# Whole-block additions on VectorE, angles and decays behind z's first gated block, and another order of the GLA value products

## The chip, the cores and the metric

The kernel runs on one core of one Trainium2 chip. The metric is the device time of one execution in microseconds, as the median over runs. The five engines are TensorE (PE in the profile, PEld its weight loads), VectorE (DVE), ScalarE (ACT), GpSimd (POOL) and SyncE (SP), which here issues nearly all transfers.

## What is computed

One layer of a decoder trunk over 1024 tokens of width 1024, in fp32. A normalized input h is projected by one wide matrix; three mixers run on pieces of the projection (sliding-window attention, gated linear attention, or GLA, and a Mamba-2 scan, or SSD); their gated outputs are projected, merged with sigmoid gates and projected once more. Cut to what the change touches:

```python
h = rms_norm(x, norm_g)
proj = h @ w_in
(aq, ak, av, ag, gq, gk, gv, gg, gdown, sxbc, sdt, sz, mg) = jnp.split(proj, split_points, axis=-1)
q = apply_rope(rms_norm(aq.reshape(b, s, ATTN_HEADS, ATTN_HEAD_DIM), attn_q_norm), cos, sin)
k = apply_rope(rms_norm(ak.reshape(b, s, ATTN_KV_HEADS, ATTN_HEAD_DIM), attn_k_norm), cos, sin)
...
o_b = gated_linear_attention(gq, gk, gv, log_alpha)
dt = jax.nn.softplus((sdt + ssd_dt_bias).astype(jnp.float32))
y_c = ssd_scan(xh, dt, a_head, sb, sc)
y_c = gated_group_rms_norm(y_c, sz, ssd_out_norm, SSD_GROUPS)
```

## The kernel before

**Products.** fp32 products are made of three fp32r products each: a matrix is split into a rounded part (hi) and the remainder (lo), and hi*hi, lo*hi and hi*lo are summed in PSUM. `split` (line 259) makes the weights' parts `wh_...` (a cast, mostly on ScalarE, line 262) and `wl_...` (a subtraction, on VectorE or GpSimd, line 265). h itself is kept as hi and lo in four blocks, `hb["11"]`, `"12"`, `"21"` and `"22"`: the first digit is the half of the width, the second the half of the tokens.

**Seven products for eight.** Most wide projections multiply 2x2 blocks with seven block products (Strassen-Winograd) instead of eight. For that they need sums of h's blocks: `block_sums` (line 489) builds t1 = 12 - 11, t3 = 22 - 12 and t2 = 22 - t1, and the loop under `zp` (line 524) builds t4n = 21 - t2, each for four slices k of 128 rows. `whole` (line 480) adds hi and lo of a slice back to the full value; `block_diff` (line 483) subtracts two, has ScalarE cast the result to `ht_hi` (line 486) and VectorE form `ht_lo` (line 487). Twelve of the `whole` calls in `block_sums` and four of the eight under `zp` run on GpSimd, the other four on VectorE.

**Order of the stages.** Input and norm; keys and values (`ps_kv`); the first query projection (`dense_tm`, line 475); the second query projection, by slices of the weight (`dense_tm_by_k`, line 293, tiles `ps_tm`, `wh_tm`, `wl_tm`); the gate z (`dense_pair_tm`, line 376, called at line 530, tiles `ps_p_z`); the rotary angles (`rope`, lines 533 to 562, 47 small VectorE operations and two sines on ScalarE); the SSD decays (`sd`, lines 565 to 593, with two small TensorE products `pacs` and `pacsT`); then the attention in eight token tiles (line 596 on), under which the scheduler lays the GLA values (line 757, `ps_p_gv`), merge gates (`mg`) and the SSD's convolved inputs (`cv`). For each attention tile `prepare` (line 607) squares, normalizes and rotates q and k, casts them to `qh` and transposes them on TensorE (`qT`); scores are `psc`, transposed weights `pT`, outputs `ppv`.

**dense_pair_tm.** It loads four weight blocks a11, a12, a21, a22 of 512 KB into three rotating buffers, makes the combinations s1 to s4 on GpSimd, and runs p1, p2, p6, p7, p4, p5, p3, each 48 matmuls of 128x256 with two PSUM banks. There are four banks (`psd1`), so that a product waits for the eviction of the product before the last. a12 is loaded twice, for p2 and for s4. z's results are evicted by `acc` (line 409, VectorE) or a copy (line 418, ScalarE), and gated by `z_block` (line 516) with a tanh on ScalarE and a multiplication on VectorE (line 520).

**What sets the order.** The program is traced in the order of the code, and a scheduler in the framework sets each engine's order of instructions from a simulation of its own when the program is built; `tc.issue_after(ins)` adds the rule that what is traced inside stands behind `ins` on that instruction's engine. Each engine, and SyncE with its transfers, then runs its list strictly in order.

Of the kernel before, what the change touches and what calls it, by code (L numbers as in the profile page):

```python
# [81 lines left out]
def kernel(  # L82
# [433 lines left out]
    def z_block(col, tok, blk):  # L516
        for i in range(2):
            th = half_tile(f"zth{col}{tok}{i}")
            A.activation(out=th, in_=blk[i], func=AF.Tanh, scale=0.5)
            V.scalar_tensor_tensor(out=blk[i], in0=th, scalar=1.0, in1=blk[i], op0=ALU.add, op1=ALU.mult)  # L520
        store_tm(z_d, col, tok, blk)

    with tc.tile_pool(name="zp", bufs=NZ) as zp:
# [12 lines left out]
        ang, a2, pr, rr, fs = (rope[:, i] for i in range(5))
        a1 = wpool.tile([P, NT, 32], F32R, tag="w2", bufs=NW2, name="a1")
        V.tensor_tensor(out=ang, in0=posf.unsqueeze(2).to_broadcast([P, NT, 32]),
                        in1=rowv[:, R_IF : R_IF + 32].unsqueeze(1).to_broadcast([P, NT, 32]), op=ALU.mult)
        V.tensor_scalar(out=a1, in0=ang, scalar1=1.0, scalar2=0.0, op0=ALU.mult, op1=ALU.add)  # L540
        V.tensor_tensor(out=a2, in0=ang, in1=a1.bitcast(F32), op=ALU.subtract)

        def frac(v):
            V.tensor_scalar(out=rr, in0=v, scalar1=MAGIC_ROUND, scalar2=MAGIC_ROUND, op0=ALU.add, op1=ALU.subtract)
            V.tensor_tensor(out=v, in0=v, in1=rr, op=ALU.subtract)

        first = True
        for a, i in ((a2, 3), (a1, 4), (a2, 2), (a1, 3), (a2, 1), (a1, 2), (a2, 0), (a1, 1), (a1, 0)):
            av = a.bitcast(F32) if a is a1 else a
            tgt = fs if first else pr  # L550
            V.tensor_scalar(out=tgt, in0=av, scalar1=C2PI[i], scalar2=None, op0=ALU.mult)
            frac(tgt)
            if a is a1 and i == 0:
# [4 lines left out]
        V.tensor_scalar(out=pr, in0=fs, scalar1=0.25, scalar2=None, op0=ALU.add)
        for v, dst in ((fs, 1), (pr, 0)):
            frac(v)  # L560
            V.tensor_scalar(out=v, in0=v, scalar1=0.49999997, scalar2=-0.49999997, op0=ALU.min, op1=ALU.max)
            A.activation(out=cs[:, dst], in_=v, func=AF.Sin, scale=6.2831855)
# [6 lines left out]
    nacs = dcyp.tile([P, NT, 8], F32, name="nacs")
    sd = wpool.tile([P, 512], F32, tag="w2", bufs=NW2, name="sd")  # L570
    dz, da, de, dw, dl = (sd[:, 64 * i : 64 * i + 64].rearrange("p (t h) -> p t h", h=8) for i in range(5))
    ah, acsT = sd[:, 320:328], sd[:64, 384:512]
    A.activation(out=ah, in_=rowv[:, R_AL : R_AL + 8], func=AF.Exp)
    V.tensor_tensor(out=dz, in0=gdt[:, :, 16:24], in1=rowv[:, R_DTB : R_DTB + 8].unsqueeze(1).to_broadcast([P, NT, 8]), op=ALU.add)
    V.scalar_tensor_tensor(out=da, in0=dz, scalar=-1.0, in1=dz, op0=ALU.mult, op1=ALU.min)
# [641 lines left out]
```

## Time and profile before

| | |
|---|---|
| Runs shown | 998.83 us median of 3 (997.33 to 1000.13) |
| Profiled execution | 995.0 us, span 993.3 us |
| PE busy | 943.2 us (95%), mean granted clock 0.985 |
| DVE busy | 757.2 us (76%) |
| ACT busy | 450.7 us (45%) |
| POOL busy | 490.3 us (49%) |
| DMA | 150.14 MB, mean 151 GB/s |

The span is what the profiler saw of one execution; the execution's own time lies 1.7 us around it. Busy is the time in which an engine ran an instruction, so a share says nothing of what a late instruction costs: that is read from the waits, stage by stage. The granted clock is TensorE's share of its full speed.

### The profile page before, as it was taken

The page shows a single profiled execution, that of the slowest core. Times are in us where ns is not written, and L with a number is a line of the kernel's source. Part 1 is how long each engine was busy: PE and PEld are TensorE (multiplying, and loading weights), DVE is VectorE, ACT ScalarE, POOL GpSimd, SP SyncE. Part 2 cuts the span into 40 slices and gives each one's busy share as a digit, 9 for nine tenths or more (in the row PEclk, how much of TensorE's full clock was granted, in tenths as well). Part 3 has the DMA queues.
Part 4 walks back from the last instruction along what each step waited for, and adds up shares of the span by engine and source line. Part 5 has one row for each costly group of instructions (what it writes and reads, how often), then busy time and mean ns, then how long its engine had stood idle before and what let it go on. Part 6 is the DMA issues. An engine that isn't in the chain of part 4 may idle for free.

```text
span 993.3 us, 14841 instructions
## 1 busy us (share of the span) xinstructions
PE 943.2 (95%) x5089; PEld 793.5 (80%) x5089; DVE 757.2 (76%) x1228; ACT 450.7 (45%) x1014; POOL 490.3 (49%) x442
## 2 busy tenths in 40 slices
PE   8989897999999999999999999999998999997998
PEld 7989897988867777778778887878886878875786
DVE  6899856777998988887887758667868754599644
ACT  6433434366566556557455555344445411133221
POOL 5765256755562672444365654444532001256775
PEclk9998997999999999999999999999999999999999
DMA  9402151423232322231596645356365866763543
GB/s 371 176 25 75 66 186 41 142 89 111 78 119 91 106 91 99 87 127 42 192 303 191 205 138 160 126 182 191 117 216 192 282 234 214 248 204 100 167 146 116
DMA packets 84410, 150.14 MB, mean 151 GB/s; under 512 B 7328, under 2 KB 40304, under 8 KB 84336
## 3 DMA queue, kind: packets, MB, share of 16 engines
q1 hardware_dynamic: 84160, 149.18, 45.3%
q8 instruction: 40, 0.66, 0.3%
q14 instruction: 34, 0.28, 0.1%
q10 hardware_dynamic: 176, 0.02, 0.0%
HBM read 101.96 MB, written 47.22 MB: 150 GB/s over the span
## 4 chain that ended last, share of the span: by engine, by line
PE 30%; DVE 16%; DMA 11%; issue 8%; ACT 6%; POOL 6%; SPq 0%; POOLq 0%; DVEq 0%; ACTq 0%
PE ps_p_mg L320 10%; PE ps_p_o L320 5%; PE ps_p_ag L320 4%; DMA tg<-tg_d 3%; DVE acc L749 2%; PE ps_p_gqk L320 2%; PE ps_p_cv L320 2%; PE ps_u L1104 1%; DMA tl<-t_d 1%; DVE sc L680 1%; DMA t_d<-tg 1%; DMA yc_r<-yc_d 1%; ACT sc L690 1%; DVE c_mg L340 1%; DVE wl_p_mg L265 1%
## 5 line engine op out<-in xcount | busy, mean ns | idle before, releaser
L320 PE MATMUL ps_p_mg<-ht_hi,wh_p_mg 128*128 128x512 f32 x192 | 75.9, 395 | 0.0
L320 PE MATMUL ps_p_mg<-ht_hi,wl_p_mg 128*128 128x512 f32 x192 | 75.8, 396 | 0.1
L320 PE MATMUL ps_p_mg<-ht_lo,wh_p_mg 128*128 128x512 f32 x192 | 75.7, 394 | 0.0
L340 DVE TENSOR_TENSOR c_mg<-ps_p_mg,c_mg 128x512 f32<-128x512 f32 x84 | 56.2, 680 | 12.4 <-PE ps_p_mg L320 7.8
L265 POOL TENSOR_TENSOR wl_p_mg<-s_mg,wh_p_mg 128x512 fp32r<-128x512 f32 x24 | 33.6, 1402 | 55.7 <-ACT wh_p_mg L262 55.6
L265 POOL TENSOR_TENSOR wl_u<-wr_u,wh_u 128x512 fp32r<-128x512 f32 x8 | 10.6, 1328 | 98.1 <-ACT wh_u L262 98.0
L320 PE MATMUL ps_p_mg<-h_hi,wl_p_mg 128*128 128x512 f32 x144 | 57.1, 396 | 0.0
L320 PE MATMUL ps_p_mg<-h_lo,wh_p_mg 128*128 128x512 f32 x144 | 56.7, 393 | 0.0
L320 PE MATMUL ps_p_mg<-h_hi,wh_p_mg 128*128 128x512 f32 x144 | 56.5, 392 | 0.0
L1107 DVE SCALAR_TENSOR_TENSOR tg<-tg,ps_u 128x512 f32<-128x512 f32 x48 | 31.7, 681 | 29.1 <-DMA tg<-tg_d 20.1
L262 ACT CAST wh_p_mg<-s_mg 128x512 fp32r<-128x512 f32 x48 | 29.6, 617 | 50.3 <-POOL s_mg L332 32.1
L265 DVE TENSOR_TENSOR wl_p_mg<-wr_mg,wh_p_mg 128x512 fp32r<-128x512 f32 x36 | 37.3, 1041 | 15.7 <-ACT wh_p_mg L262 8.9
L749 DVE SCALAR_TENSOR_TENSOR acc<-c_cv,cwh,acc 128x512 f32<-128x512 f32 (+3 forms) x48 | 41.8, 888 | 5.0 <-ACT acc L746 4.8
L320 PEld LDWEIGHTS ps_p_mg<-ht_hi,wl_p_mg 128*128 128x128 f32 x192 | 36.1, 188 | 7.9 <-DVE wl_p_mg L265 0.7
L320 PEld LDWEIGHTS ps_p_mg<-ht_lo,wh_p_mg 128*128 128x128 f32 x192 | 36.1, 188 | 7.1
L320 PEld LDWEIGHTS ps_p_mg<-ht_hi,wh_p_mg 128*128 128x128 f32 x192 | 36.1, 188 | 7.1
L690 ACT ACTIVATE sc<-sc,nm 128x256 f32<-128x256 f32 (+1 forms) x64 | 30.9, 484 | 19.7 <-DVE nm L685 19.6
L342 DVE SCALAR_TENSOR_TENSOR c_o<-ps_p_o,c_o 128x512 f32<-128x512 f32 x28 | 18.9, 688 | 26.6 <-POOL c_o L346 16.0
L262 ACT CAST wh_u<-wr_u 128x512 fp32r<-128x512 f32 x24 | 14.7, 620 | 48.7 <-PE ps_u L1104 39.2
L733 ACT ACTIVATE c_mg<-c_mg 128x1024 f32<-128x1024 f32 x24 | 25.3, 1056 | 15.6 <-DVE c_mg L340 12.8
L320 PEld LDWEIGHTS ps_p_mg<-h_lo,wh_p_mg 128*128 128x128 f32 x144 | 27.1, 188 | 5.4
L320 PEld LDWEIGHTS ps_p_mg<-h_hi,wl_p_mg 128*128 128x128 f32 x144 | 27.1, 188 | 5.3
(478 smaller groups left out, 3444.9 us busy)
## 6 DMA issues: line engine op xcount, KB each, us to landing
wr_mg<-in_w_fm_dram SPq DMA_DIRECT2D x24, 512.0 KB, 3.9
tg_d<-c_mg SPq DMA_DIRECT2D x24, 512.0 KB, 2.6
tg<-tg_d SPq DMA_DIRECT2D x24, 512.0 KB, 4.4
wr_u<-in_w_br_dram SPq DMA_DIRECT2D x24, 256.0 KB, 3.8
xq<-in_xf_dram SPq DMA_DIRECT2D x8, 512.0 KB, 10.9
wr_cv<-in_w_fm_dram SPq DMA_DIRECT2D x8, 512.0 KB, 3.5
xbc_d<-acc SPq DMA_DIRECT2D x16, 256.0 KB, 2.4
e<-acs_dram SPq DMA_DIRECT2D x16, 256.0 KB, 5.5
```

The lines of the kernel that those rows point to most:

```text
L262: A.copy(hi[:, :n], raw)
L265: (lo_eng or V).tensor_tensor(out=lo[:, :n], in0=raw, in1=hi[:, :n].bitcast(F32), op=ALU.subtract)
L320: T.matmul(ps, lhsT=l[:, k, :], rhs=r, start=n == 0, stop=n == 3 * kt - 1)
L340: V.tensor_tensor(out=o, in0=p, in1=c, op=op)
L342: V.scalar_tensor_tensor(out=o, in0=p, scalar=scale, in1=c, op0=ALU.mult, op1=op)
L680: V.tensor_tensor_reduce(out=sc[:, 2 * pr2 + j, :nk], in0=psc[:, 256 * j : 256 * j + nk], in1=mk, scale=1.0, scalar=-3.0e38, op0=ALU.add, ...
L690: A.activation(out=sc[:, j, :nk], in_=sc[:, j, :nk], func=AF.Exp, bias=nm[:, h : h + 1], accum_out=dn[:, h : h + 1])
L733: A.activation(out=c, in_=c, func=AF.Tanh, scale=0.5)
L749: V.scalar_tensor_tensor(out=acc[:, z:], in0=r[:, o + z - d : o + 512 - d], scalar=cwh[:, 4 * c + 3 - d : 4 * c + 4 - d], in1=acc[:, z:], ...
L1104: T.matmul(ps, lhsT=l[:, k, :], rhs=r, start=m_ == 0, stop=m_ == 11)
L1107: V.scalar_tensor_tensor(out=o, in0=o, scalar=1.0, in1=ps, op0=ALU.add, op1=ALU.mult)
```

## The change

It does three things. `whole` runs on VectorE in all its sixteen GpSimd calls. The angles and the decays are put behind the second gated half of z's first block (`z_gated[1]`) on VectorE's list. And `dense_pair_tm`, when it makes the GLA values, takes its products in the order p1, p6, p7, p4, p2, p5, p3, starts from a11, a21 and a22, and loads a12 once, behind the evictions of p4; on SyncE's list that load stands behind the decays' store and the first attention tile's loads. Blocks that are only indented are cut.

```diff
@@ -385,7 +385,11 @@
                 G.tensor_tensor(out=o[i], in0=a[i], in1=b[i], op=op)
             return o
 
-        a11, a12, a21 = load(0, "a11"), load(1, "a12"), load(2, "a21")
+        a11 = load(0, "a11")
+        if c == C_SZ:
+            a12, a21 = load(1, "a12"), load(2, "a21")
+        else:
+            a21, a22 = load(2, "a21"), load(3, "a22")
 
         def mul(w, key, nm):
             parts = [split(w[i], 512, f"{nm}{i}_{name}", True, G if nm in (Z_LO if c == C_SZ else GV_LO) else None, work) for i in range(2)]
@@ -412,6 +416,33 @@
             t = st_tile(f"{nm}_{name}")
             return [t[:, :512], t[:, 512:]]
 
+        if c != C_SZ:
+            s3 = combs([work(F32, f"s3{i}_{name}") for i in range(2)], a11, a21, ALU.subtract)
+            s1 = combs(a21, a21, a22, ALU.add)
+            c11 = block("c11")
+            p1 = mul(a11, "11", "p1")
+            for i in range(2):
+                A.copy(c11[i], p1[i])
+            s2 = combs(a11, s1, a11, ALU.subtract)
+            c12 = block("c12")
+            acc(c12, mul(s2, "t2", "p6"), c11)
+            c22 = block("c22")
+            acc(c22, mul(s3, "t3", "p7"), c12)
+            p4 = mul(a22, "t4n", "p4")
+            c21 = block("c21")
+            acc(c21, p4, c22)
+            evac(1, 0, c21)
+            a12 = load(1, "a12")
+            acc(c11, mul(a12, "21", "p2"), c11)
+            evac(0, 0, c11)
+            p5 = mul(s1, "t1", "p5")
+            acc(c22, p5, c22)
+            evac(1, 1, c22)
+            acc(c12, p5, c12)
+            s4 = combs(a12, a12, s2, ALU.subtract)
+            acc(c12, mul(s4, "22", "p3"), c12)
+            evac(0, 1, c12)
+            return
         c12 = block("c12")
         p1 = mul(a11, "11", "p1")
         for i in range(2):
@@ -477,8 +508,8 @@
     dense_tm_by_k(C_Q + 1, spill_tm(qkv_d, 256))
 
 
-    def whole(o, key, k, eng):
-        eng.tensor_tensor(out=o, in0=hb[key][0][:, k, :].bitcast(F32), in1=hb[key][1][:, k, :].bitcast(F32), op=ALU.add)
+    def whole(o, key, k):
+        V.tensor_tensor(out=o, in0=hb[key][0][:, k, :].bitcast(F32), in1=hb[key][1][:, k, :].bitcast(F32), op=ALU.add)
 
     def block_diff(o, a, b, key, k):
         V.tensor_tensor(out=o, in0=a, in1=b, op=ALU.subtract)
@@ -489,9 +520,9 @@
     def block_sums(k):
         f, g = st_tile(f"fa{k}"), st_tile(f"fb{k}")
         f1, f2, f3 = f[:, :512], f[:, 512:], g[:, :512]
-        whole(f1, "11", k, G)
-        whole(f2, "12", k, G)
-        whole(f3, "22", k, G)
+        whole(f1, "11", k)
+        whole(f2, "12", k)
+        whole(f3, "22", k)
         block_diff(f1, f2, f1, "t1", k)
         block_diff(f2, f3, f2, "t3", k)
         block_diff(f3, f3, f1, "t2", k)
@@ -517,80 +548,84 @@
         for i in range(2):
             th = half_tile(f"zth{col}{tok}{i}")
             A.activation(out=th, in_=blk[i], func=AF.Tanh, scale=0.5)
-            V.scalar_tensor_tensor(out=blk[i], in0=th, scalar=1.0, in1=blk[i], op0=ALU.add, op1=ALU.mult)
+            z_gated.append(V.scalar_tensor_tensor(out=blk[i], in0=th, scalar=1.0, in1=blk[i], op0=ALU.add, op1=ALU.mult))
         store_tm(z_d, col, tok, blk)
+
+    z_gated = []
 
     with tc.tile_pool(name="zp", bufs=NZ) as zp:
         with tc.high_priority():
             for k in range(4):
                 f1, f2 = (zp.tile([P, 512], F32, tag="zf", bufs=3, name=f"f{i}{k}") for i in "cd")
-                whole(f1, "t2", k, G)
-                whole(f2, "21", k, V)
+                whole(f1, "t2", k)
+                whole(f2, "21", k)
                 block_diff(f1, f2, f1, "t4n", k)
         dense_pair_tm(C_SZ, z_block, "z", lambda dt, nm: zp.tile([P, 512], dt, tag="z2", name=nm))
 
 
-        posf = const.tile([P, NT], F32, name="posf")
-        V.tensor_copy(posf, posi)
...
+        with tc.issue_after(z_gated[1].ins):
+            posf = const.tile([P, NT], F32, name="posf")
+            V.tensor_copy(posf, posi)
...
-    acs_dram = dram.tile([64, P], F32, name="acs_dram")
...
+    with tc.issue_after(z_gated[1].ins):
+        acs_dram = dram.tile([64, P], F32, name="acs_dram")
...
+        Q.dma_start(acs_dram, acsT)
```

How it moves instructions, as the two built programs list them. First ScalarE at the second query projection; `wh_tm_1` to `wh_tm_3` are its weights' rounded parts, `ht_hi` the casts of block differences. Before:

```order
L486 CAST ht_hi<-fb_1054 128x512
L486 CAST ht_hi<-fa_1067 128x512
L262 CAST wh_p_z<-wr_a_z 128x512 x2
L486 CAST ht_hi<-fa_1067 128x512
L467 COPY spl<-ps_tm_10_700 128x512
L486 CAST ht_hi<-fb_1068 128x512
L486 CAST ht_hi<-fa_1081 128x512
L262 CAST wh_tm_1_865<-wr_tm_0_805 128x512
L262 CAST wh_tm_2_917<-wr_tm_1_807 128x512
L262 CAST wh_tm_3_969<-wr_tm_1_807 128x512
L486 CAST ht_hi<-fa_1081 128x512
```

Now:

```order
L517 CAST ht_hi<-fb_1054 128x512
L262 CAST wh_p_z<-wr_a_z 128x512 x2
L498 COPY spl<-ps_tm_10_700 128x512
L262 CAST wh_tm_1_865<-wr_tm_0_805 128x512
L262 CAST wh_tm_2_917<-wr_tm_1_807 128x512
L517 CAST ht_hi<-fa_1067 128x512
L262 CAST wh_tm_3_969<-wr_tm_1_807 128x512
L517 CAST ht_hi<-fa_1081 128x512
L517 CAST ht_hi<-fa_1067 128x512
L262 CAST wh_p_z<-wr_a_z 128x512 x2
L517 CAST ht_hi<-fa_1081 128x512
L517 CAST ht_hi<-fb_1068 128x512
```

`wh_tm_1` and `wh_tm_2` now stand ahead of every cast of `fa_1067`, `fb_1068` and `fa_1081`, the third and fourth slices, and `wh_tm_3` behind one of them.

VectorE, before, in the block sums ahead of `wl_tm_1`, where the first angle operation (`rope`) stands:

```order
L484 TENSOR_TENSOR fa_1067<-fa_1067 128x512
L487 TENSOR_TENSOR ht_lo<-fb_1054,ht_hi 128x512
L538 TENSOR_TENSOR rope<-posf,rowv 128x256
L481 TENSOR_TENSOR fd_1103<-h_hi,h_lo 128x512
L484 TENSOR_TENSOR fa_1067<-fb_1068,fa_1067 128x512
L487 TENSOR_TENSOR ht_lo<-fa_1067,ht_hi 128x512
L265 TENSOR_TENSOR wl_p_z<-wr_a_z,wh_p_z 128x512 x2
```

Now, at z's first evictions (line 413) and gatings (line 551), behind which the angles and decays begin:

```order
L518 TENSOR_TENSOR ht_lo<-fc_1123,ht_hi 128x512
L498 COPY spl<-ps_tm_1_810 128x512
L498 COPY spl<-ps_tm_3_812 128x512
L413 TENSOR_TENSOR c_z<-ps_p_z_1206,c_z 128x512
L551 SCALAR_TENSOR_TENSOR c_z<-zth_1258,c_z 128x512
L413 TENSOR_TENSOR c_z<-ps_p_z_1231,c_z 128x512
L551 SCALAR_TENSOR_TENSOR c_z<-zth_1261,c_z 128x512
L568 CAST posf<-posi 128x8
L572 TENSOR_TENSOR rope<-posf,rowv 128x256
L413 TENSOR_TENSOR c_z<-ps_p_z_1284,c_z 128x512
L574 TENSOR_SCALAR a_1611<-rope 128x256
L609 TENSOR_TENSOR sd<-gdt,rowv 128x64
```

All of `rope` and `sd` now stands behind two gatings; before, all of it stood ahead of the first eviction of z, but for the last three operations of the decays. Of the sixteen additions fourteen stand ahead of `wl_tm_1` on VectorE's list now, and none is left on GpSimd's.

TensorE, where the first attention tile's transposes come. Before, behind 108 GLA value matmuls:

```order
L403 MATMUL ps_p_gv_3094<-wl_p_gv,ht_hi 128x256
L403 MATMUL ps_p_gv_3094<-wh_p_gv,ht_hi 128x256
L403 MATMUL ps_p_gv_3094<-wh_p_gv,ht_lo 128x256
L403 MATMUL ps_p_gv_3094<-wl_p_gv,ht_hi 128x256
L648 MATMUL qT_2_1733<-identr,qh_2_1730 128x128 x4
L648 MATMUL qT_0_1742<-identr,qh_0_1739 128x128 x4
L648 MATMUL qT_1_1751<-identr,qh_1_1748 128x128 x4
L677 MATMUL psc_0_0_1762<-kT,qT_1729 128x128 x4
L677 MATMUL psc_0_1_1769<-kT,qT_1729 128x128 x4
```

Now, behind 215:

```order
L407 MATMUL ps_p_gv_3191<-wl_p_gv,h_hi 128x256
L407 MATMUL ps_p_gv_3191<-wh_p_gv,h_hi 128x256
L683 MATMUL qT_2_1733<-identr,qh_2_1730 128x128
L407 MATMUL ps_p_gv_3191<-wh_p_gv,h_lo 128x256
L407 MATMUL ps_p_gv_3191<-wl_p_gv,h_hi 128x256
L407 MATMUL ps_p_gv_3191<-wh_p_gv,h_hi 128x256
L407 MATMUL ps_p_gv_3191<-wh_p_gv,h_lo 128x256
L407 MATMUL ps_p_gv_3191<-wl_p_gv,h_hi 128x256
L407 MATMUL ps_p_gv_3216<-wh_p_gv,h_lo 128x256
L683 MATMUL qT_2_1733<-identr,qh_2_1730 128x128 x3
L683 MATMUL qT_0_1742<-identr,qh_0_1739 128x128 x4
```

Behind this place the attention's transposes are laid between fewer matmuls of the GLA values, gates and convolved inputs; its last `ppv` stands before the same `gqk` matmuls in both lists.

## Rows read from the trace of the kernel before

**Rows 1.** Busy time by stage: us, each engine busy (xcount), PE clock, DMA share, GB/s

```profile
44.80:69.50 24.70, 24.70 (x203) 24.54 (x201) 23.51 (x22) 7.32 (x14) 20.88 (x13) 1.00 0.07 22
69.50:95.00 25.50, 19.58 (x145) 19.33 (x145) 25.33 (x41) 10.26 (x18) 12.57 (x9) 0.87 0.26 83
95.00:141.90 46.90, 43.02 (x341) 42.19 (x340) 35.66 (x65) 17.31 (x29) 19.81 (x15) 0.96 0.34 107
141.90:181.00 39.10, 33.15 (x249) 32.36 (x249) 27.09 (x64) 16.95 (x48) 26.45 (x34) 0.87 0.22 71
181.00:455.00 274.00, 267.54 (x1423) 215.37 (x1422) 233.89 (x463) 159.44 (x371) 136.59 (x129) 1.00 0.31 101
455.00:993.30 538.30, 514.24 (x2432) 420.42 (x2430) 378.74 (x517) 213.00 (x486) 245.60 (x205) 0.99 0.56 183
```

**Rows 2.** TensorE's waits, 25 to 215 us: releaser, us in total, times, longest

```profile
PE qT L648 <- ACT qh L644: 4.3, 1, 4.3
PE ps_tm L308 <- ACT wh_tm L262: 3.4, 1, 3.4
PE ps_tm L308 <- DVE wl_tm L265: 2.5, 1, 2.5
PE ps_p_z L403 <- DVE c_z L409: 1.9, 1, 1.9
PE qT L648 <- DVE qh L645: 1.3, 2, 1.1
PE ps_p_z L403 <- POOL wl_p_z L265: 1.2, 2, 0.7
PE ps_p_z L403 <- ACT c_z L418: 0.8, 1, 0.8
PE pacsT L591 <- DVE acs_t L587: 0.4, 1, 0.4
```

**Rows 3.** TensorE in order of time: start us, us, instruction, idle before it

```profile
75.97 0.58 PE L308 MATMUL ps_tm<-wl_tm,h_hi 128*128 128x256 f32 x1 [2.54 <-DVE wl_tm L265]
...
80.19 0.36 PE L308 MATMUL ps_tm<-wh_tm,h_hi 128*128 128x256 f32 x1
...
95.01 0.28 PE L403 MATMUL ps_p_z<-wh_p_z,h_hi 128*128 128x256 f32 x1
...
159.90 0.37 PE L648 MATMUL qT<-identr,qh 128*128 128x128 f32 x1 [4.26 <-ACT qh L644]
...
165.08 0.52 PE L403 MATMUL ps_p_gv<-wh_p_gv,ht_hi 128*128 128x256 f32 x1
...
169.19 1.00 PE L677 MATMUL psc<-kT,qT 128*128 128x128 f32 x8
```

**Rows 4.** Line 481, whole-block additions: xcount, ns min/median/max, first to last start

```profile
L481 POOL TENSOR_TENSOR fa<-h_hi,h_lo x8: 1671/1740/1766, 25.4 to 62.2; 128x512 f32<-128x512 f32 x8
...
L481 DVE TENSOR_TENSOR fd<-h_hi,h_lo x4: 678/682/1781, 64.1 to 100.7; 128x512 f32<-128x512 f32 x4
```

**Rows 5.** VectorE in order of time, three remainders without GpSimd beside them

```profile
42.91 1.88 DVE L236 TENSOR_TENSOR h_lo<-xq,h_hi 128x512 fp32r<-128x512 f32 x3
```

**Rows 6.** ScalarE in order of time, at wh_tm and at the first attention tile

```profile
71.73 0.62 ACT L486 CAST ht_hi<-fa 128x512 fp32r<-128x512 f32 x1
...
72.26 1.66 ACT L262 CAST wh_tm<-wr_tm 128x512 fp32r<-128x512 f32 x3
...
148.41 0.74 ACT L620 ACTIVATE t<-qk 128x640 f32<-128x640 f32 x1 [2.18 <-PE ps_p_gv L403]
...
159.44 0.71 ACT L644 CAST qh<-qk 128x256 fp32r<-128x256 f32 x2 [8.81 <-DVE qk L632]
```

**Rows 7.** 60 to 150 us, instructions of tile rope (first) and sd (second) alone

```profile
60.00:150.00 90.00, 24.33 (x47) 0.83 (x2) 0.94 0.30 94
...
60.00:150.00 90.00, 0.33 (x2) 0.30 (x2) 5.00 (x9) 0.98 (x4) 0.94 0.30 94
```

**Rows 8.** Line 715, TensorE's weight loads of the attention's last products

```profile
L715 PEld LDWEIGHTS ppv<-pT,vv x120: 132/136/137, 189.9 to 440.8; 128*64 128x64 f32 x120
```

More of the change, by code (lines that the diff above doesn't have):

```diff
@@ L536 @@
[L536 to L553, printed above, removed]
-                frac(tgt)
-            if not first:
-                V.tensor_tensor(out=fs, in0=fs, in1=pr, op=ALU.add)
-            first = False
@@ L558 @@
[L558 to L562, printed above, removed]
-    acs_dram = dram.tile([64, P], F32, name="acs_dram")
-    dt_t = dcyp.tile([P, NT, 8], F32, name="dt_t")
-    acs_t = dcyp.tile([P, NT, 8], F32, name="acs_t")
-    eacs_t = dcyp.tile([P, NT, 8], F32, name="eacs_t")
@@ L569 @@
[L569 to L575, printed above, removed]
@@ L584 @@
-    V.scalar_tensor_tensor(out=da, in0=dt_t, scalar=-1.0, in1=ah.unsqueeze(1).to_broadcast([P, NT, 8]), op0=ALU.mult, op1=ALU.mult)
-    pa = mtile("pacs")
-    T.matmul(pa[:, :64], lhsT=triu, rhs=da.rearrange("p t h -> p (t h)"), start=True, stop=True)
-    V.tensor_copy(acs_t.rearrange("p t h -> p (t h)"), pa[:, :64])
-    A.activation(out=eacs_t, in_=acs_t, func=AF.Exp)
-    V.tensor_single_scalar(out=nacs, in_=acs_t, scalar=-1.0, op=ALU.mult)
-    pb = mtile("pacsT")
-    T.transpose(pb[:64, :P], acs_t.rearrange("p t h -> p (t h)"), ident)
@@ new lines @@
+    with tc.issue_after(z_gated[1].ins):
+        acs_dram = dram.tile([64, P], F32, name="acs_dram")
+        dt_t = dcyp.tile([P, NT, 8], F32, name="dt_t")
+        acs_t = dcyp.tile([P, NT, 8], F32, name="acs_t")
+        eacs_t = dcyp.tile([P, NT, 8], F32, name="eacs_t")
+        nacs = dcyp.tile([P, NT, 8], F32, name="nacs")
+        sd = wpool.tile([P, 512], F32, tag="w2", bufs=NW2, name="sd")
+        dz, da, de, dw, dl = (sd[:, 64 * i : 64 * i + 64].rearrange("p (t h) -> p t h", h=8) for i in range(5))
+        ah, acsT = sd[:, 320:328], sd[:64, 384:512]
+        A.activation(out=ah, in_=rowv[:, R_AL : R_AL + 8], func=AF.Exp)
+        V.tensor_tensor(out=dz, in0=gdt[:, :, 16:24], in1=rowv[:, R_DTB : R_DTB + 8].unsqueeze(1).to_broadcast([P, NT, 8]), op=ALU.add)
+        V.scalar_tensor_tensor(out=da, in0=dz, scalar=-1.0, in1=dz, op0=ALU.mult, op1=ALU.min)
+        A.activation(out=de, in_=da, func=AF.Exp)
+        V.tensor_single_scalar(out=dw, in_=de, scalar=1.0, op=ALU.add)
+        A.activation(out=dl, in_=dw, func=AF.Ln)
+        A.activation(out=da, in_=dl, func=AF.Exp, scale=-1.0)
+        V.scalar_tensor_tensor(out=dw, in0=dw, scalar=-1.0, in1=de, op0=ALU.add, op1=ALU.subtract)
+        V.tensor_tensor(out=dw, in0=dw, in1=da, op=ALU.mult)
+        V.tensor_tensor(out=dl, in0=dl, in1=dw, op=ALU.subtract)
+        V.scalar_tensor_tensor(out=dt_t, in0=dz, scalar=0.0, in1=dl, op0=ALU.max, op1=ALU.add)
+        V.scalar_tensor_tensor(out=da, in0=dt_t, scalar=-1.0, in1=ah.unsqueeze(1).to_broadcast([P, NT, 8]), op0=ALU.mult, op1=ALU.mult)
+        pa = mtile("pacs")
+        T.matmul(pa[:, :64], lhsT=triu, rhs=da.rearrange("p t h -> p (t h)"), start=True, stop=True)
+        V.tensor_copy(acs_t.rearrange("p t h -> p (t h)"), pa[:, :64])
+        A.activation(out=eacs_t, in_=acs_t, func=AF.Exp)
+        V.tensor_single_scalar(out=nacs, in_=acs_t, scalar=-1.0, op=ALU.mult)
+        pb = mtile("pacsT")
+        T.transpose(pb[:64, :P], acs_t.rearrange("p t h -> p (t h)"), ident)
+        V.tensor_copy(acsT, pb[:64, :P])
+        Q.dma_start(acs_dram, acsT)
```

36 lines of the change are left out of this document (25 added, 11 removed).

## Prediction

> **What bounds the kernel now.** I read the busy time by stage first [rows 1]. TensorE (PE) works 943.2 of 993.3 us (table above), so only its idle time and its time at the lower clock can be won. From 44.8 to 69.5 us it never rests. From 69.5 to 95.0 (the rest of the second query projection) it is idle 25.50 - 19.58 = 5.9 us, from 95.0 to 141.9 (z's seven products) 46.90 - 43.02 = 3.9 us, and from 141.9 to 181.0 (the GLA values and the first attention tile) 39.10 - 33.15 = 5.9 us; in the three the mean granted clock falls to 0.87, 0.96 and 0.87. From 181 to 455 it idles 6.5 us in 274, and 24.1 behind that, where the change alters nothing but the order of a few SSD matmuls. So what the change can win lies between 69.5 and 181.
>
> The list of what TensorE waited for names each loss [rows 2]: 3.4 us for ScalarE's cast wh_tm and 2.5 for VectorE's remainder wl_tm (second query projection); 1.9, 1.2 and 0.8 in z; 0.4 for acs_t; 4.3 + 1.3 for the first tile's qh. Sum 15.8. After two of these waits TensorE runs at the 1.2 GHz level [rows 3]: the 19 matmuls from 75.97 to 80.19 (a first row and the row behind the last) take 4.22 us, the 19 GLA matmuls from 165.08 to 169.19 take 4.11. At full clock 203 matmuls take 24.70 us [rows 1], 0.12 each, so 19 take 2.3: 1.9 and 1.8 us are lost. In z the clock of 0.96 over 46.9 us bounds the loss at 1.9; I take 1.5. Everything together: 15.8 + 1.9 + 1.8 + 1.5 = **21.0 us**.
>
> The cause of the first two waits is VectorE (DVE), busy 23.51 of 24.70 us and then all 25.5 [rows 1], since 16 additions on GpSimd (POOL) run beside it. The same 128x512 addition of two SBUF tiles takes 0.68 us on VectorE when undisturbed and 1.78 when not; on GpSimd it takes 1.74 [rows 4]. Three in a row take 1.88, so one costs 0.60 in sequence [rows 5]. The ScalarE cast wh_tm at 72.26 needs nothing from VectorE, but stands behind a cast of a block difference, at 71.73, that does [rows 6].
>
> **Additions to VectorE.** Each leaves GpSimd and gives back up to 1.78 - 0.68 = 1.10 us to a neighbour, and costs 0.60: from -0.50 to +0.60 each, -8.0 to +9.6 us of VectorE for 16. I take the gain, because the same form shows both durations. By the order, VectorE now has 31 operations of this size and three small copies between the last h_lo (44.8 us) and wl_tm_1, with nothing on GpSimd: 31 x 0.60 + 0.3 = 18.9, so wl_tm_1 is written near 64.3, where TensorE now gets it at 75.97 [rows 3]. ScalarE's wh_tm_1 now stands before the late casts. Both are ready before TensorE asks at 69.5: **-3.4 - 2.5 - 1.9 = -7.8 us**, and z begins at 95.01 - 7.8 = 87.2.
>
> The Trainium skill (Perfetto Trace Analysis, Optimizing Scalar/DVE Operations) speaks against this step: where VectorE is saturated, work may be moved off it, even to GpSimd, though the two share a port and it might not help. By its first half the sum would get +9.6 us on VectorE; the two durations of one form bear out its caveat instead. The skill's State Buffer page (Who interferes with whom) says that the loser waits for the other's whole instruction; that would give back 1.74 per addition, the trace shows 1.10.
>
> **Angles and decays held until z's first gated blocks.** 47 + 9 VectorE operations, 24.3 + 5.0 us, some of them stretched [rows 7], ran from 62 us on, between the block sums and ahead of z's evictions. Now the evictions stand first. The waits in z came from that: TensorE waited for evictions of p1 and p2 to free PSUM. With z starting at 87.2 and 48 x 0.12 = 5.8 us per product, p1's banks are wanted at 98.7, p2's at 104.5, 4 us or more after their evictions can run. I take all of z: **-3.9 - 1.5 = -5.4 us**, at worst half of it. z then ends at 87.2 + 336 x 0.12 = 127.5.
>
> What it costs: between about 101 and 148 us VectorE has these 29.3 us and some 30 evictions, gatings and weight remainders of 0.6 (18 us). acs_t, on which TensorE's transpose pacsT waits, is queued behind z's last evictions and most of the angles. TensorE comes to pacsT at 127.5 + 28 x 0.12 = 130.9; I put acs_t at 134: **+3** (0 to 5). Queued behind it is wl_p_gv of GLA's second product, **+1** (0 to 3). ScalarE's queue gains no work.
>
> **First attention tile.** TensorE's order puts its first transpose behind 215 of the 336 GLA value matmuls instead of 108. The old wait of 4.3 + 1.3 and its slow clock go: **-5.6 - 1.8 = -7.4**. The transpose comes at 127.5 + 215 x 0.12 = 153.3, plus the 4 us above 157. From the tile's square to its qh cast it is 159.44 - 148.41 = 11.0 us [rows 6]; the sine table, its input, is late now, near 143, so qh comes at 154 to 160: **+3** (0 to 7).
>
> **GLA products reordered.** One 512 KB weight load goes away; the DMA share in these stages is 0.22 to 0.34 [rows 1], so 0. The load of a12 stands later on SP's queue, behind the first tile's loads, but p2 is now the fifth product, 144 matmuls or 17 us later: 0. Lost pace in the attention behind it: 107 matmuls x 0.12 = 12.8 us less filler between the same first and last attention matmul, with VectorE already 233.9 of 274 us busy [rows 1]: **+2** (0 to 8).
>
> **Sum.** -21.0 (written above as 7.8 + 5.4 + 7.4 with 0.4 for pacsT) + 3 + 1 + 3 + 2 = **-12.0 us**. The profiled execution took 995.0 us (span 993.3): 983.0. The median of the runs shown is 998.83, 3.8 above it: **986.8 us**. With every new wait at 0 it is 977.8; with all at their upper end (23 us) 1000.8.
>
> **Rivals.**
> 1. The attention gives it back. From its first transpose at 159.90 [rows 3] to its last ppv at 440.8 [rows 8] it took 281 us, with TensorE waiting little, which speaks for TensorE as its pace; VectorE at 85% on the mean, and ScalarE and GpSimd waiting on it in chains, speak against. If the chains set most of the pace, the first transpose at 157 wins only 3 us and some compression: 991 to 999, middle 996. Chance 0.24, half of it within the bound of 0.3% (3 us), which is what a measurement here can tell from no change.
> 2. Slower: the first tile comes late and the attention keeps its 281 us. Place: TensorE's first qT transpose. It decides at 159.9 us: each us behind that lengthens the run. With the upper ends 5 + 3 + 7 it starts near 168, 8 us late: 1007. For it: 29 us of VectorE work now stand directly ahead. Against: the 4 to 6 us of margin worked out above. Chance 0.06.
> 3. Slower: VectorE is saturated and its neighbours do not get shorter. The 14 additions that stand ahead of wl_tm_1 then push it by 14 x 0.60 = 8.4 us, to 84.4, and TensorE waits that much longer: some 1003 to 1007. Against it stands the form with both durations, whose short cases fall where GpSimd rests. The Trainium skill's advice above on a saturated VectorE would end here; the rows bear it out poorly. Chance 0.04.
>
> That the change does not do what it says is excluded by the order: the additions are gone from GpSimd, and the angles stand behind the second gated block.
>
> **How the numbers follow.** The forecast has 0.66: 977 to 993, likeliest 987. Faster by over 0.3% (below 995.8): 0.66 + 0.12 = 0.78; within it: 0.12; slower (above 1001.8): 0.10. A range of 977 to 997 leaves out rivals 2 and 3, a quarter of rival 1 and the lucky edge, some 0.19.
>
> **What would show it.** Right: no TensorE wait for wh_tm or wl_tm and clock 1.00 from 69.5 on; the first z matmul near 87; VectorE's additions at 0.68; z ending near 128; a wait of a few us at pacsT; the first qT near 157 to 160; the attention's last matmul near 429, 12 us before 440.8. Wrong: additions or their neighbours at 1.78, z's PSUM waits still there, or the attention's end back at 441.

## The result, and the profile after

The change takes 988.66 us (median of four runs) against 998.92 for the kernel before: ratio 0.9884, 95% interval 0.9862 to 0.9905. A second measurement, beside some of the experiments, gave 0.9913 (0.9881 to 0.9945). The forecast was 986.8 us, with a range of 977 to 997. The profiled execution's span fell from 993.3 to 983.7 us.

Busy time by stage, after; the columns are those of [rows 1] and the stretches are the same:

```profile
44.80:69.50 24.70, 24.70 (x204) 24.70 (x203) 24.70 (x45) 10.83 (x20) 0.33 (x1) 1.00 0.23 74
69.50:95.00 25.50, 25.50 (x215) 25.50 (x214) 19.42 (x20) 7.35 (x15) 19.61 (x10) 1.00 0.19 68
95.00:141.90 46.90, 42.44 (x340) 42.05 (x339) 42.77 (x81) 17.35 (x32) 19.74 (x15) 0.96 0.29 99
141.90:181.00 39.10, 37.58 (x308) 36.69 (x307) 29.13 (x67) 17.33 (x43) 28.92 (x32) 1.00 0.35 117
181.00:455.00 274.00, 267.73 (x1356) 211.66 (x1355) 232.71 (x465) 164.94 (x383) 139.46 (x131) 0.99 0.29 95
455.00:983.70 528.70, 503.41 (x2376) 412.61 (x2374) 370.15 (x510) 207.35 (x476) 237.60 (x200) 0.98 0.55 184
```

Against [rows 1], TensorE's idle time from 69.5 to 95 is gone and the clock there is 1.00. VectorE does 45 operations in the 24.70 us before, where it did 22. From 95 to 141.9 TensorE idles 4.5 us against 3.9, but 1.9 of the 4.5 are the wait for pacsT, which now falls into this stretch; in z itself it waits 2.6. VectorE works 42.77 us there instead of 35.66. From 141.9 to 181 TensorE idles 1.5 us instead of 5.9.

What TensorE waited for from 25 to 215 us, after (us in total, times, longest), for [rows 2]:

```profile
PE ps_p_z L407 <- DVE c_z L413: 2.6, 1, 2.6
PE pacsT L626 <- DVE acs_t L622: 1.9, 1, 1.9
PE qT L683 <- ACT qh L679: 0.8, 1, 0.8
PE ps_p_gv L407 <- POOL wl_p_gv L265: 0.7, 1, 0.7
```

And from 181 us to the end, the longest three:

```profile
PE pu L952 <- ACT bk L940: 5.1, 2, 4.9
PE ps_p_gqk L320 <- DVE wl_p_gqk L265: 4.0, 1, 4.0
...
PE ppv L750 <- DVE pT L744: 3.6, 1, 3.6
```

The first and last z matmul, pacsT and the first qT on TensorE's timeline, after (start, duration), for [rows 3]:

```profile
87.22 0.28 PE L407 MATMUL ps_p_z<-wh_p_z,h_hi 128*128 128x256 f32 x1
...
131.70 0.28 PE L407 MATMUL ps_p_z<-wl_p_z,h_hi 128*128 128x256 f32 x1
...
137.46 0.30 PE L626 MATMUL pacsT<-ident,acs_t 128*64 128x128 f32 x1 [1.91 <-DVE acs_t L622]
...
161.96 0.28 PE L683 MATMUL qT<-identr,qh 128*128 128x128 f32 x1 [0.84 <-ACT qh L679]
```

The loads for ppv (ns, first and last start), for [rows 8]:

```profile
L750 PEld LDWEIGHTS ppv<-pT,vv x120: 132/136/230, 198.2 to 435.5; 128*64 128x64 f32 x120
```

z begins 7.8 us earlier than before. The first attention transpose comes 2.1 us **later** than before (159.90), and yet the attention ends 5.3 us earlier. Part of that is what stands in it. From the first qT to the last ppv TensorE ran these matmuls of the GLA query and key product, `ps_p_gqk`, before and after (us, busy, count, clock, DMA share, GB/s):

```profile
159.90:441.00 281.10, 10.69 (x45) 0.98 0.31 101
161.96:435.70 273.74, 18.70 (x78) 0.99 0.31 103
```

The GLA value matmuls in the same stretch went from 228 (30.4 us) to 121 (15.4), so the two together take 7.0 us less, and the stretch is 7.4 us shorter. The section on the change says that the last `ppv` stands before the same `gqk` matmuls in both lists; the traces show 33 more of them ahead of it now.

The additions, all on VectorE now (ns minimum, median, maximum), for [rows 4]:

```profile
L512 DVE TENSOR_TENSOR fa<-h_hi,h_lo x8: 674/679/681, 27.6 to 59.5; 128x512 f32<-128x512 f32 x8
L512 DVE TENSOR_TENSOR fb<-h_hi,h_lo x4: 678/680/682, 45.9 to 62.5; 128x512 f32<-128x512 f32 x4
L512 DVE TENSOR_TENSOR fc<-ht_hi,ht_lo x4: 679/680/1776, 57.7 to 80.9; 128x512 f32<-128x512 f32 x4
L512 DVE TENSOR_TENSOR fd<-h_hi,h_lo x4: 678/1175/1777, 58.3 to 84.4; 128x512 f32<-128x512 f32 x4
```

17 of these 20 take 0.68 us; the other three stand among GpSimd's sums for z.

**An account of the span.** TensorE runs the same 5089 matmuls in all these kernels, so what differs is mostly its idle time and what it loses at the 1.2 GHz level. I take idle time from the table by stage, and half of TensorE's busy time in stretches at clock 0.50 as the loss. This table holds it for every kernel run (us); "rest of span" is what is left, the work as the profile counts it. It differs by up to 6.4 us between kernels, which the account does not explain.

| Kernel | to 181 | 181 to 455 | behind 455 | rest of span | span |
|---|---|---|---|---|---|
| before | 27.3 | 6.5 | 27.3 | 932.2 | 993.3 |
| full change | 11.5 | 9.3 | 32.2 | 930.7 | 983.7 |
| full change, again | 12.2 | 8.7 | 32.7 | 930.6 | 984.2 |
| additions alone | 18.2 | 7.5 | 26.6 | 932.0 | 984.4 |
| additions alone, again | 19.6 | 6.6 | 28.3 | 931.6 | 986.1 |
| hold alone | 23.4 | 9.5 | 39.8 | 936.1 | 1008.9 |
| GLA order alone | 24.2 | 9.3 | 29.5 | 934.8 | 997.8 |
| additions and hold | 15.9 | 8.9 | 37.5 | 937.0 | 999.4 |
| additions and GLA order | 19.1 | 7.7 | 25.7 | 934.7 | 987.2 |
| hold and GLA order | 19.2 | 7.8 | 32.8 | 931.5 | 991.2 |
| additions twice | 34.1 | 7.4 | 27.0 | 931.0 | 999.5 |
| additions, pacs early | 16.2 | 7.3 | 28.7 | 936.5 | 988.7 |
| full, pacs early | 12.9 | 8.1 | 33.9 | 932.2 | 987.1 |
| full, bk on VectorE | 12.2 | 8.8 | 34.4 | 931.1 | 986.5 |

The full change wins 15.8 us ahead of 181, then loses 2.8 between 181 and 455 and 4.9 behind that (1.2 of idle time, 3.7 at the lower clock). With 1.5 less in the last part that makes 9.6.

### The profile page after: what moved, and what is told of

It is laid out like the page before. It is cut to its first block, busy times and chain, and to the rows that moved or that the text cites. A ratio compares the mean times of both kernels' runs of the same rounds, so it can differ in the third digit from the quotient of the medians.

```text
span 983.7 us, 14826 instructions
## 1 busy us (share of the span) xinstructions
PE 942.4 (96%) x5089; PEld 792.5 (81%) x5089; DVE 750.8 (76%) x1244; ACT 451.6 (46%) x1014; POOL 471.5 (48%) x426
## 4 chain that ended last, share of the span: by engine, by line
PE 33%; DVE 13%; DMA 9%; issue 7%; POOL 5%; ACT 4%; SPq 0%; POOLq 0%; DVEq 0%; ACTq 0%
PE ps_p_mg L320 10%; PE ps_p_o L320 5%; PE ps_p_ag L320 4%; DMA tg<-tg_d 3%; PE ps_p_gqk L320 3%; PE ps_p_cv L320 2%; PE ps_u L1139 1%; DMA e<-acs_dram 1%; PE ps_p_gg L320 1%; DVE acc L784 1%; DMA tl<-t_d 1%; DVE tg L1142 1%; DVE sc L715 1%; DMA yb_r<-ybg_d 1%; PE py L963 1%
## 5 line engine op out<-in xcount | busy, mean ns | idle before, releaser
L262 ACT CAST wh_p_mg<-s_mg 128x512 fp32r<-128x512 f32 x48 | 29.5, 615 | 49.6 <-POOL s_mg L332 28.9
L265 DVE TENSOR_TENSOR wl_p_mg<-wr_mg,wh_p_mg 128x512 fp32r<-128x512 f32 x36 | 31.6, 877 | 14.3 <-ACT wh_p_mg L262 6.9
L725 ACT ACTIVATE sc<-sc,nm 128x256 f32<-128x256 f32 (+1 forms) x64 | 30.9, 486 | 11.1 <-DVE nm L720 11.1
L320 PEld LDWEIGHTS ps_p_mg<-h_hi,wh_p_mg 128*128 128x128 f32 x144 | 27.1, 188 | 5.2
```

The lines of the kernel that those rows point to most:

```text
L262: A.copy(hi[:, :n], raw)
L265: (lo_eng or V).tensor_tensor(out=lo[:, :n], in0=raw, in1=hi[:, :n].bitcast(F32), op=ALU.subtract)
L320: T.matmul(ps, lhsT=l[:, k, :], rhs=r, start=n == 0, stop=n == 3 * kt - 1)
L725: A.activation(out=sc[:, j, :nk], in_=sc[:, j, :nk], func=AF.Exp, bias=nm[:, h : h + 1], accum_out=dn[:, h : h + 1])
```

## The experiments

### The three parts, each alone and in pairs

The edits are parts of the diff: `whole` on VectorE, the two `issue_after` blocks, and the branch for the GLA values in `dense_pair_tm`. A part that is left out is undone so (the GLA branch is deleted whole, and a11, a12, a21 are loaded first):

```diff
-        V.tensor_tensor(out=o, in0=hb[key][0]...
+        eng.tensor_tensor(out=o, in0=hb[key][0]...
-        with tc.issue_after(z_gated[1].ins):
+        if True:
-        if c != C_SZ:
```

**Additions alone** (no hold, old GLA order): 

> The kernel before with the whole-block additions on VectorE alone; angles, decays and the GLA order as before. Theory (each part carries its own term): no TensorE wait for wh_tm or wl_tm, clock 1.00 from 69.5 on, z begins near 87.2, the additions take 0.68 us where GpSimd rests; z's waits (3.9 us) and the first tile's (5.6 us and its slow clock) stay, so 7 to 8 us are won: 991 to 993. Rival (the hold carries the gain): the angles still run between the block sums, VectorE now has all the additions as well, wl_tm stays late, z begins at 92 or later: 996 to 1003.

**Hold alone**: 

> The kernel before with the hold of angles and decays alone. Theory: the waits for wh_tm and wl_tm stay (additions and their neighbours still at 1.7 us beside GpSimd), z begins at 93 to 95; z loses about 2 us, the first tile's wait goes since its transposes stand behind 198 GLA matmuls: 993 to 997. Rival (the hold carries the gain): with the angles' operations out of the block sums VectorE is in time, z begins by 89, and the time is within 1.5 us of the full change, 987 to 990.

**GLA order alone**: 

> The kernel before with the new order of the GLA products alone. Theory: no term but a few us at most: the first tile's transposes stand behind 124 instead of 108 GLA matmuls, 16 x 0.12 = 1.9 us of its 4.3 us wait filled: 996 to 999. Rival (the order brings the first tile's gain): the wait for qh and its slow clock go, 991 to 994.

**Hold and GLA order**: 

> The full change without its whole-block additions. Theory: the full change's 988.7 plus the 7.8 us of the second query projection: 995 to 997, with waits for wh_tm and wl_tm of 4 us or more in the trace. Rival (the hold carries the gain): 988 to 991 and z begins by 89.

**The full change again, and the additions alone again**, on one chip: 

> The full change again, beside the whole-block additions alone on the same chip. Theory, after the first four runs (the additions carry the gain; the hold and the GLA order win in z and at the first tile and give it back by a first tile that comes 10 us later and by stalls behind the attention): within 2 us of the additions alone, ratio to before 0.987 to 0.991. Rival (the sum predicted, 4 us of it from hold and order): at least 3 us faster than the additions alone.

> The whole-block additions alone, again. Theory: ratio to before 0.989 to 0.993, and within 2 us of the full change. Rival: 3 us or more slower than the full change.

**Additions and GLA order**: 

> Additions and GLA order, without the hold. Theory: the order alone changed nothing (ratio 1.001) and does not here either, 987 to 990; the first tile's transposes stand behind 124 GLA matmuls and start near 154 to 156. Rival (the order takes out the first tile's wait once the table is early): qh wait and slow clock gone, 983 to 986, faster than the full change.

**Additions and hold**: 

> Additions and hold, with the old order of the GLA products. Theory (what the hold costs behind the first tile comes from its own order of the attention, whatever the block sums do; alone it cost 11.6 us and the additions win 7 to 9): 996 to 1002, attention from first transpose to last output product 284 us or more. Rival (the hold cost only because z began late behind the block sums): 986 to 990, attention 273 to 281 us.

Measured, as ratios to the kernel before (95% interval); the last three columns are times of the traces in us, from z's first matmul to its last, the first qT, and from there to the last ppv:

| Additions | Hold | GLA order | ratio | z | first qT | attention |
|---|---|---|---|---|---|---|
| no | no | no | 1 | 46.5 | 159.9 | 280.9 |
| yes | no | no | 0.9909 (0.9875 to 0.9943) | 44.4 | 151.8 | 281.8 |
| yes, again | no | no | 0.9928 (0.9902 to 0.9953) | 44.4 | 151.7 | 281.4 |
| no | yes | no | 1.0116 (1.0086 to 1.0147) | 40.2 | 170.5 | 285.6 |
| no | no | yes | 1.0011 (0.9996 to 1.0026) | 46.5 | 164.0 | 279.3 |
| yes | yes | no | 1.0053 (1.0031 to 1.0075) | 40.2 | 161.9 | 286.7 |
| yes | no | yes | 0.9926 (0.9902 to 0.9950) | 47.1 | 155.8 | 280.1 |
| no | yes | yes | 0.9958 (0.9940 to 0.9975) | 42.0 | 170.0 | 272.3 |
| yes | yes | yes | 0.9884 (0.9862 to 0.9905) | 44.5 | 162.0 | 273.5 |
| yes, again | yes | yes | 0.9913 (0.9881 to 0.9945) | 44.8 | 161.9 | 273.3 |

What follows. **The additions carry the gain**: alone they give all of it that can be measured (0.9913 for the full change against 0.9928 on the same chip, the intervals overlapping). Their time of 987.8 us lies below the 991 to 993 expected, in part because the kernel before ran at 997.4 beside it; the win, 9.6 us there and 8.1 in the repeat, is a little over the 7 to 8 expected. With them z begins at 87.1 and everything behind it comes about 8 us earlier, as a block; without them it begins at 95 or later, so the rival that the hold would mend the block sums falls. **The hold alone costs 1.2%**, against both its expectations: it does clear z (40.2 us, 336 x 0.12 without a wait) but the first tile comes 6 to 11 us later in each pair with and without it, and by the account most of its cost stands behind 455 (39.8 us lost against 27.3). **The GLA order does nothing alone, and is worth 1.4 to 1.7% beside the hold** (1.0053 to 0.9913 or 0.9884). The three parts do not add up; my theory that each carries its own term falls, and with it what I expected of the hold alone (993 to 997). The GLA order alone, and additions with GLA order, came out as the theory expected and their rivals fall: qh is still waited for (2.4 and 3.6 us). Hold and GLA order have the waits for wh_tm (3.6 us) and wl_tm (2.5) back, as expected, but lie only 0.5 to 0.7% behind the full change: 993.0 us, where 995 to 997 was expected. For "additions and hold" the theory formed after the first runs holds, 1.0053 where 996 to 1002 us was expected, and 286.7 us of attention.

### Why the hold gained nothing in z

With hold and additions z is free of waits; the GLA order brings one back. VectorE's and GpSimd's timelines around z's fourth product, in the full change:

```profile
111.85 1.52 DVE L579 TENSOR_TENSOR rope<-rope 128x256 f32<-128x256 f32 x1
...
115.95 0.68 DVE L413 TENSOR_TENSOR c_z<-ps_p_z,c_z 128x512 f32<-128x512 f32 x1
...
117.37 1.26 DVE L578 TENSOR_SCALAR rope<-rope 128x256 f32<-128x256 f32 x1
...
119.97 1.78 DVE L265 TENSOR_TENSOR wl_p_gv<-wr_a_gv,wh_p_gv 128x512 fp32r<-128x512 f32 x1
...
122.01 1.75 DVE L265 TENSOR_TENSOR wl_p_gv<-wr_a_gv,wh_p_gv 128x512 fp32r<-128x512 f32 x1
123.68 0.68 DVE L413 TENSOR_TENSOR c_z<-ps_p_z,c_z 128x512 f32<-128x512 f32 x1
...
115.70 2.78 POOL L385 TENSOR_TENSOR s_gv<-wr_a_gv 128x512 f32<-128x512 f32 x2 [2.61 <-DMA wr_a_gv<-in_w_tm_dram]
118.44 2.75 POOL L385 TENSOR_TENSOR wr_a_gv<-wr_a_gv 128x512 f32<-128x512 f32 x2
```

and with additions and hold, in the old GLA order:

```profile
111.50 0.41 DVE L548 TENSOR_TENSOR rope<-rope 128x256 f32<-128x256 f32 x1
...
115.29 1.80 DVE L265 TENSOR_TENSOR wl_p_gv<-wr_a_gv,wh_p_gv 128x512 fp32r<-128x512 f32 x1
...
118.30 1.77 DVE L265 TENSOR_TENSOR wl_p_gv<-wr_a_gv,wh_p_gv 128x512 fp32r<-128x512 f32 x1
...
120.33 0.68 DVE L409 TENSOR_TENSOR c_z<-ps_p_z,c_z 128x512 f32<-128x512 f32 x1
...
116.49 3.04 POOL L265 TENSOR_TENSOR wl_p_gv<-wr_a_gv,wh_p_gv 128x512 fp32r<-128x512 f32 x2
134.63 1.71 POOL L385 TENSOR_TENSOR s_gv<-wr_a_gv 128x512 f32<-128x512 f32 x1 [15.10 <-DMA z_d<-c_z]
```

In the old order GpSimd's sums for GLA start at 134.63, when z is done. In the new one a21 and a22 are loaded first and the sums start at 115.70. The same eviction c_z, behind angles and GLA remainders on VectorE's list, then runs at 123.68 instead of 120.33; TensorE waits 2.56 us for it, and runs at clock 0.50 from 126.0 to 129.4. The 3.35 us have three parts. z started 0.3 later. Another 1.2 are there at the eviction before (115.95 against 114.49), ahead of the sums: an angle operation takes 1.52 instead of 0.41 us beside a second half of wl_p_z that GpSimd now makes earlier. The last 1.9 come beside the sums: two angle operations of 0.78 and 1.39 us where they take 0.28 and 0.41 elsewhere, and one more of 0.41 ahead of the eviction. The two GLA remainders take 1.8 us in both kernels. So with the additions the hold gains 4.2 us in z (44.4 to 40.2) and the order takes 4.3 back (44.5); without them it is 6.3 and 1.8. That the order costs z its gain is shown by these pairs; that earlier work on GpSimd is how is read from the rows and was not tried by itself. The same rows show what GpSimd does not touch: the eviction at 115.95, with one operand in PSUM, takes 0.68 us beside a sum on GpSimd.

### Is it GpSimd's port or GpSimd's chain?

The additions on VectorE as in the kernel with them alone, and the twelve of `block_sums` a second time on GpSimd, into a free half of a tile:

```diff
         whole(f1, "11", k)
+        G.tensor_tensor(out=g[:, 512:], in0=hb["11"][0][:, k, :].bitcast(F32), in1=hb["11"][1][:, k, :].bitcast(F32), op=ALU.add)
...
```

> The additions on VectorE as in the kernel with them alone, and twelve of them a second time on GpSimd, into a half tile that nothing reads: the same chain on VectorE, with GpSimd busy beside it. Theory (VectorE was late because its operations last 1.7 instead of 0.68 us beside GpSimd's): additions and their neighbours at 1.7 us again, VectorE later than in the kernel before, waits for wh_tm or wl_tm back, z begins at 95 or later, 996 to 1010. Rival (VectorE was late because it waited in series for results of GpSimd that took 1.74 us each): z begins near 87, no such waits, 986 to 990.

Measured: ratio 1.0071 (1.0051 to 1.0090), so slower than the kernel before. Its additions on VectorE, the copies on GpSimd, and TensorE's two waits in the second query projection:

```profile
L481 DVE TENSOR_TENSOR fa<-h_hi,h_lo x8: 679/1684/1780, 29.7 to 72.4; 128x512 f32<-128x512 f32 x8
L481 DVE TENSOR_TENSOR fb<-h_hi,h_lo x4: 676/1224/1780, 51.1 to 75.4; 128x512 f32<-128x512 f32 x4
```

```profile
L493 POOL TENSOR_TENSOR fb<-h_hi,h_lo x4: 1677/1680/1749, 25.8 to 65.5; 128x512 f32<-128x512 f32 x4
```

```profile
PE ps_tm L308 <- ACT wh_tm L262: 5.5, 1, 5.5
...
PE ps_tm L308 <- DVE wl_tm L265: 2.9, 1, 2.9
```

VectorE waits for no result of these copies, and yet 9 of its 20 additions take 1.7 us again (2 with the additions alone), both waits are back and longer, and z begins at 98.35. From the last h_lo to wl_tm_1 VectorE runs 36 operations at 0.85 us each; in the kernel with the additions alone 35 at 0.55, in the kernel before 30 at 1.02. The run is not clean in one point: the scheduler put one more cast ht_hi ahead of wh_tm on ScalarE's list (7 where the additions alone have 6), so a part of that wait comes through the order; this cast itself waits 11.1 us for VectorE. In the kernel before, too, VectorE stood idle for a GpSimd sum only once in 25 to 85 us:

```profile
DVE fa L484 <- POOL fa L481: 1.1, 1, 1.1
```

The theory holds, and the chain through GpSimd as the main cause falls.

### Where the win ahead of the attention goes

Behind the attention the full change waits 4.9 us at the first pu of the SSD, against 1.1 in the kernel before and 0.8 with the additions alone. TensorE's timeline there, in the full change:

```profile
494.50 0.48 PE L320 MATMUL ps_p_mg<-ht_hi,wl_p_mg 128*128 128x512 f32 x1
...
495.28 0.39 PE L320 MATMUL ps_p_mg<-ht_hi,wl_p_mg 128*128 128x512 f32 x1
500.55 0.79 PE L952 MATMUL pu<-xd,bk 128*128 128x256 f32 x1 [4.88 <-ACT bk L940]
```

and with the additions alone:

```profile
494.99 0.48 PE L320 MATMUL ps_p_mg<-ht_lo,wh_p_mg 128*128 128x512 f32 x1
...
498.75 0.39 PE L320 MATMUL ps_p_mg<-ht_hi,wl_p_mg 128*128 128x512 f32 x1
499.97 1.13 PE L921 MATMUL pu<-xd,bk 128*128 128x256 f32 x4 [0.83 <-ACT bk L909]
```

4 gate matmuls stand between pb and pu in the full change, 17 with the additions alone (and 17 in the kernel before): the scheduler left less filler there. bk is copied by ScalarE at 500.15, behind a cast that waits for GpSimd. The last run moves that copy to VectorE:

```diff
-            A.copy(bk.rearrange("p g n -> p (g n)"), pb[:, :256])
+            (V.tensor_copy if t == 0 else A.copy)(bk.rearrange("p g n -> p (g n)"), pb[:, :256])
```

> The full change, with the copy of the first SSD tile's bk out of PSUM on VectorE instead of ScalarE, where it stands behind casts and exponentials; TensorE's order is the same up to and behind the first pu. Theory (what the hold wins ahead of the attention is lost behind it, a good part of it at the first pu, which waits 4.9 us for bk and then runs at the lower clock): the wait shrinks to 2 to 3 us, bounded by xd, the slow stretch shrinks, 2 to 4 us won: 983 to 986. Rival (another operand is as late, or the loss shows up again behind it): pu waits as long as before, or the time stays at 987 to 989.

Measured: ratio 0.9899 (0.9871 to 0.9926), no change against the full change. The first pu starts at 494.98 and waits only 0.7 us, for xd; but now:

```profile
PE ps_p_mg L320 <- ACT c_mg L354: 2.4, 1, 2.4
PE pu L952 <- ACT bk L940: 1.8, 2, 1.4
...
PE pu L952 <- DVE xd L931: 0.7, 1, 0.7
```

The wait went to the next work of ScalarE (an eviction c_mg) and to the second pu, and the loss behind 455 is 34.4 us instead of 32.2 or 32.7. The second half of the rival holds: the loss shows up again behind it, so the wait for this bk is not by itself what costs the time. Other waits, such as the 4.0 us for wl_p_gqk, were not tried.

In the additions with the hold and the old GLA order, the loss there is larger still. Two rows of TensorE's waits, and one of SyncE's, in that kernel:

```profile
PE px L892 <- DMA zin<-z_d: 5.7, 1, 5.7
PE ps_p_gqk L320 <- DVE mn L839: 2.9, 1, 2.9
```

```profile
SPq L846 <- ACT eb L845: 10.2, 1, 10.2
```

SyncE stands 10.2 us for ScalarE's eb, so that the SSD's loads behind it start at 500 (487 in the full change), and the first px waits for them and then runs at clock 0.50 from 505.8 to 519.4. That this follows from the attention's later end (448.6 against 435.5) is read from the trace; it was not tried by itself. The attention is 13 us longer there mostly because more stands in it: from the first qT to the last ppv 17 more GLA value matmuls than in the full change, 10 more of the merge gates and 6 more gqk, about 8.4 us by their starts. So the length of the attention is no measure of its pace where the scheduler fills it differently.

### An earlier pacs

Two attempts on the wait at pacsT. With the additions alone, the two products get high priority and stand behind z's second product:

```diff
+        with tc.high_priority(), tc.issue_after(marks["p2", "z"].ins):
             pa = mtile("pacs")
...
```

> The additions alone, with the decays' two small TensorE products traced at high priority and put behind z's second product instead of behind the whole of z. Theory: the wait of 2 us at pacsT and the slow stretch behind it (about 1.7 us) go; the first tile still starts when its qh is there, at 150 to 153, behind 124 instead of 108 GLA matmuls, so half is passed on: 985 to 987. Rival (the attention's start sets the end): 987 to 989, as the additions alone.

In the full change the same, with the hold taken off the decays:

```diff
-    with tc.issue_after(z_gated[1].ins):
+    if True:
         acs_dram = dram.tile([64, P], F32, name="acs_dram")
```

> The full change, with the decays not held and their two TensorE products put forward (only the angles stay behind z's second gated half). Theory: the wait of 1.9 us at pacsT and its slow stretch go, the first tile stands behind 225 GLA matmuls and starts near 160; 984 to 987. Rival (the attention's start and VectorE's chain in it set the end): 986.5 to 989, no change against the full change.

Measured: 0.9935 (0.9912 to 0.9959) and 0.9929 (0.9902 to 0.9957): nothing won in either. The times, 990.3 and 989.4 us, lie above both expected ranges of each. In the first the wait grew, since acs_t still stands behind the angles on VectorE's list:

```profile
PE pacsT L598 <- DVE acs_t L594: 7.5, 1, 7.5
```

now inside z, which takes 50.7 us; so its edit did not do what it was for. In the second 2.9 us of wait appeared at pacs, and the first tile waits 2.3 us for qh again. No kernel run beats the full change and the additions alone by more than their intervals.

## Why the prediction was right, and where it was not

The time was right to 2 us and the direction too. By its steps:

- **Additions to VectorE, -7.8: right, and it is the result.** z was to begin at 87.2 and begins at 87.22. wl_tm_1 was to be written near 64.3; its operation runs from 64.28 to 64.96, behind 34 operations (the 31 and three small copies of the forecast) at 0.56 us each. The clock from 69.5 on is 1.00 and no wait for wh_tm or wl_tm is left. The choice of 1.10 us given back per addition, made from one form with two durations, is what the copies on GpSimd confirm from the other side. Rival 3 (a saturated VectorE) has the right place and the wrong sign; the Trainium skill (Perfetto Trace Analysis, Optimizing Scalar/DVE Operations) says that moving work off a saturated VectorE may make sense, and warns that between VectorE and GpSimd it might not help, since they share a read port. The runs here side with the warning: the additions cost 1.7 us beside GpSimd and 0.68 without it.
- **Angles and decays held, -5.4 in z: wrong.** z took 44.5 us where 40.3 were forecast; it wins 2.0 against before, and as much without the hold. The step that failed is "GLA products reordered: 0", together with taking all of z: the order puts more of GpSimd's work beside the held angles, which the working did not look at. Without the order the hold clears z as forecast (40.2 us).
- **pacsT, +3 (0 to 5): 1.9 measured. wl_p_gv, +1 (0 to 3): 0.7**, in the row of GpSimd's wl_p_gv.
- **First tile, -7.4 + 3: nearly.** The stage from 141.9 on lost 9.8 us before (5.9 idle, 3.9 slow), 1.5 after; qh is waited for 0.8 us. The forecast had put the slow part at 1.8, from the 19 GLA matmuls alone, but the clock was 0.50 from 158.9 on; so the loss to be won was larger than the 21.0 us of the forecast by about 2. The first qT came at 161.96, where 157 to 160 was forecast.
- **Attention, +2 (0 to 8): in range, on a premise that was wrong.** Its length fell by 7.4 us (280.9 to 273.5), not by 12.8 - 2, and it ended at 435.5, not at 429. But the step counts 12.8 us less filler "between the same first and last attention matmul", and the 33 gqk matmuls that came in take 8.0 us of it back. That is work from behind the attention done earlier, no loss. What was lost there by the account is 2.8: idle time from 181 to 455 is 6.3 against 6.5, but a stretch at clock 0.50 from 269.3 on cost 3.1. That the chains set the attention's pace (rival 1) is not borne out: it shortened by what its matmuls shrank by.
- **Behind the attention, 0: wrong by 5 us.** The step "the change alters nothing but the order of a few SSD matmuls" is the one that took the rest: the GLA query and key product waits 4.0 us for wl_p_gqk where its longest wait was 2.0 (for mn), pu waits 4.9 for bk where it waited 1.1, and the clock falls at both. By the account the loss there comes with the hold: kernels with it lose 32.2 to 39.8 us behind 455, kernels without it 25.7 to 29.5. Which change of the order brings it stays open.

Forecast to 181 us: -14.0; measured -15.8. Forecast behind: +2; measured +7.7, less 1.5 that the account leaves in the work. That is -12.0 against -9.6 in the span, while the medians moved by 10.3. The net of hold and order, -4.2 by the forecast, is -2.5 and -1.5 by the two pairs of ratios (0.9884 and 0.9909, 0.9913 and 0.9928), which their intervals do not tell from nothing. So the time was met because the largest term was right; the two smaller parts won about 7 us ahead of the attention (18.2 or 19.6 to 11.5 or 12.2) and gave most or all of it back behind. That more was won ahead and more lost behind than forecast, so that the errors partly cancelled, was luck.
